# Forgetting attention: key gate sums loaded in two copies, masks filled in place, blocks 2 and 3 ahead of 0 and 1

## The chip, the cores and the metric

The kernel runs on one core of one Trainium2 chip, in one launch. The metric is the time of the device in microseconds (us). The engines are called as in the profile: PE (matrix products and transposes), DVE (vector), ACT (activations, casts), POOL (general), SP (issues transfers); PEld is PE's loading of weights.

## The reference, cut to what matters

The model has two layers on 512 tokens of width 1024, all in float32: layer 0 is a dilated attention and a gated ConvFFN, layer 1 a forgetting attention and a ConvFFN. The change lies in the forgetting attention alone. It has 16 heads of 64; keys, values and the cumulative log forget gates `c` are shared and computed once:

```python
def fox_mixer(xn, w_q, w_o, k, v, c):
    q = (xn @ w_q).reshape(B, T, B_HEADS, HEAD_DIM)
    c_t = c.transpose(0, 2, 1)
    for i in range(T // BLK):                       # T = 512, BLK = 128
        q0, q1 = i * BLK, (i + 1) * BLK
        s = jnp.einsum('bqhd,bkhd->bhqk', q[:, q0:q1], k[:, :q1]) * HEAD_DIM ** -0.5
        s = s + (c_t[:, :, q0:q1, None] - c_t[:, :, None, :q1])
        causal = jnp.arange(q0, q1)[:, None] >= jnp.arange(q1)[None, :]
        s = jnp.where(causal, s, NEG)
        p = jax.nn.softmax(s, axis=-1)
        outs.append(jnp.einsum('bhqk,bkhd->bqhd', p, v[:, :q1]))
    return jnp.concatenate(outs, axis=1).reshape(B, T, B_WIDTH) @ w_o
```

The term `c[q]` is the same for all keys of a query's row, so a softmax over the row does not depend on it.

## The kernel before

Every product of two float32 matrices is made of three products of high and low parts (`mm3`, three matmuls at lines 292, 293 and 294: high with high, low with high, high with low). The order of the instructions on each engine is the order in which the program writes them; semaphores are put in between by dependences, and tiles come from pools with a fixed number of buffers (`t4` tiles of 4 KB per partition, `t2`, `t8`, and `bank`, the eight banks of PE's accumulators). A tile whose slot is still in use makes its writer wait.

Ahead of the attention the gates are summed to `c` (16 heads by 512 keys, times 8) and stored in the chip's memory as `cd` by POOL. Four transposes on PE (`cq_ps`, L1798) and a copy on DVE turn `c` to `cq`, the query's sum with the query on the partition. For each pair of heads j = 0 to 7, SP loads the two rows of `cd`, repeated on all 128 partitions, as `ck` (`load_ck`).

The attention is a loop over 16 iterations m and two more to drain it. An iteration handles two of the four query blocks of one head pair: `pairs` is (j, 0), (j, 2) for j = 0 to 7. Blocks 0 and 1 (called light here: 128 and 256 keys) are the even iterations, blocks 2 and 3 (heavy: 384 and 512 keys) the odd ones. It is a pipeline of three iterations:

- iteration m: `f_scores` (PE, tile `s_ps`, L1833), then for each block and head in `f_exp` one DVE reduction that adds the bias and takes the minimum (L1841), and ACT's exponential (L1843); `f_norm` divides by the sums on DVE (L1853);
- iteration m + 1: `f_transpose` (PE, tile `pT_ps`, L1865; ACT copies it to `pT`, L1867);
- iteration m + 2: `f_pv` (PE, tile `o_ps`, L1880), and for a pair's second half `f_out_high` (ACT) and `f_out_low` (DVE).

`f_bias(j, i)` makes the bias of a block on POOL, one iteration ahead: two TENSOR_SCALAR (L1814, one for each head) write `cq - ck` to a new `t4` tile, and one AFFINE_SELECT (L1815) fills the upper triangle of the last 128 columns with a large negative number. The reduction, the exponential and the normalisation then work in place in that tile.

Between these steps stand other works with a place of their own by m:

- `q_part`: two projections of six matmuls in each iteration, for the queries of pairs j + 1 and j + 2; `q_high` (ACT) and `q_low` (DVE) split the result in the even iterations;
- the weights of the queries and of the output projection: `W.high` (ACT cast), `W.low` (DVE difference, L69); for the queries' weights the low part is made by ACT's negative high part (L62, at an even iteration's end) and an accumulating transfer on POOL's queue (`low_added`, L86, in the odd iteration);
- `sums_between`: loads, four DVE differences and a store of `dsums` for the ConvFFN behind it;
- from m = 13 on, `po.both`: the first matmuls of the output projection.

Of the kernel before, what the change touches and what calls it, by code (L numbers as in the profile page):

```python
# [9 lines left out]
F32 = mybir.dt.float32  # L10
# [3 lines left out]
ALU = mybir.AluOpType  # L14

D = 1024
T = 512
# [6 lines left out]
NEG = -1e30  # L24
BIG = 3.0e38
# [83 lines left out]
def trunk_kernel(ctx, tc, x, norm_gains, w_qkv_a, w_o_a, w_q_b, w_o_b, kv_norm, w_kvf, b_f,  # L109
                 w_up, conv_w, conv_b, w_down, rope, out):  # L110
    nc = tc.nc
    act, dve, pool, pe, sp = nc.scalar, nc.vector, nc.gpsimd, nc.tensor, nc.sync
# [5 lines left out]
    sml = ctx.enter_context(tc.tile_pool(name="sml", bufs=6))  # L118
    psp = ctx.enter_context(tc.tile_pool(name="psp", bufs=8, space=bass.MemoryType.PSUM))

    def t8(shape, dt=F32, name="t8"):
        return p8.tile(shape, dt, tag="t8", name=name)

    def t4(shape, dt=F32, name="t4"):
        return p4.tile(shape, dt, tag="t4", name=name)

    def t2(shape, dt=F32, name="t2"):
        return p2.tile(shape, dt, tag="t2", name=name)

    def bank(shape, name="bank"):  # L130
        return psp.tile(shape, F32, tag="ps", name=name)

    def small(n, name):
        return sml.tile([128, n], F32, tag=name, name=name)
# [95 lines left out]
    W = Weights(nc, new_raw, lambda: t8([128, 2, 1024], F32R, name="w"), pieces)  # L230
# [39 lines left out]
    for b in range(1, 4):  # L270
# [5 lines left out]
    ident = cst.tile([128, 128], F32, name="ident")  # L276
# [11 lines left out]
                       fill=NEG, base=0, channel_multiplier=-1)  # L288
    pool.affine_select(mask0[:, 128:256], mask0[:, 128:256], pattern=[[-1, 128]], compare_op=ALU.is_ge,
                       fill=NEG, base=0, channel_multiplier=1)  # L290
# [76 lines left out]
    def xs(xT, kc, s):  # L367
        return xT[0][kc // 4][:, kc % 4, s], xT[1][kc // 4][:, kc % 4, s]
# [1184 lines left out]
        act.copy(hi, o)  # L1553
        dve.tensor_tensor(lo, o, hi.bitcast(F32), ALU.subtract)

    c8 = []

    def gates():

        fo = bank([128, 128], name="f_ps")  # L1560
        for kc in range(KD):
            for q in range(4):
                pe.matmul(fo[32 * q:32 * q + 32], wfg[:, kc, :],
                          bd2.nT[kc // 4][:, kc % 4, q * 128:q * 128 + 128], start=kc == 0, stop=kc == KD - 1)

        zt = t2([128, 4, 128], name="z")
        z, u, e, lg = (zt[:, i] for i in range(4))
        act.activation(z, fo, AF.Identity, bias=bfc)
        yield
        dve.tensor_scalar(u, z, -1.0, None, ALU.mult)  # L1570
        dve.tensor_tensor(u, u, z, ALU.min)
        act.activation(e, u, AF.Exp)
        yield
        dve.tensor_scalar(u, e, 1.0, None, ALU.add)
        dve.scalar_tensor_tensor(e, u, -1.0, e, ALU.add, ALU.subtract)
        dve.tensor_scalar(z, z, 0.0, None, ALU.min)
        act.activation(lg, u, AF.Ln)
        dve.reciprocal(u, u)
        yield
        dve.tensor_tensor(e, e, u, ALU.mult)  # L1580
        dve.tensor_tensor(lg, lg, e, ALU.subtract)
        zz, one = t2([16, T], name="zz"), t2([16, T], name="one")
        pool.memset(one, 1.0)
        for q in range(4):
            r = slice(32 * q, 32 * q + 16)
            dve.tensor_tensor(zz[:, q * 128:q * 128 + 128], z[r], lg[r], ALU.subtract)
        yield
        c = t2([16, T], name="c8")
        dve.tensor_tensor_scan(c, one, zz, 0.0, ALU.mult, ALU.add)
        dve.tensor_scalar(c, c, 8.0, None, ALU.mult)  # L1590
        pool.dma_start(cd, c)
        c8.append(c)
        yield


# [8 lines left out]
    xTq = [], []  # L1604
    cks = {}

    def load_ck(j, queue=sp):
        t = t4([128, 2, T], name="ck")
        s = cd[2 * j:2 * j + 2, :]
        queue.dma_start(t, bass.AP(tensor=s.tensor, offset=s.offset, ap=[[0, 128], [T, 2], [1, T]]))  # L1610
        cks[j] = t

    qT = {}
    qps = {}
# [1 line left out]
    def q_part(j, i):  # L1616

        if j >= 8:
            return
        if i == 0:  # L1620
            qps[j] = (bank([128, T], name="q_ps"), [t.rearrange("p (k c) -> p k c", k=8) for t in W.get()])
        o, (wh, wl) = qps[j]
        for kc in (2 * i, 2 * i + 1):
            bh, bl = xs(xTq, kc, ALL)
            mm3(o, wh[:, kc, :], wl[:, kc, :], bh, bl, kc == 0, kc == KD - 1)
# [128 lines left out]
    for bp in range(2):  # L1754
        for s in range(2):
            t = slice(bp * 128, bp * 128 + 128)
# [17 lines left out]
    for c in range(4, 8):  # L1774
# [18 lines left out]
            next(gate)  # L1793
        if c == 6:
            next(down1)
    cqp = bank([128, 4, 16], name="cq_ps")
    for b in range(4):
        pe.transpose(cqp[:, b, :], c8[0][:, b * 128:(b + 1) * 128], ident[:16, :16])  # L1798
    cq = sml.tile([128, 4, 16], F32, tag="cq", name="cq", bufs=1)
    dve.tensor_copy(cq, cqp)  # L1800
    next(down1)
    load_ck(0)


    prob = {}

    bia = {}

    def f_bias(j, i):
        n = (i + 1) * 128  # L1810
        bias = t4([128, 2, T], name="bias")
        for hh in range(2):
            hd = 2 * j + hh
            pool.tensor_scalar(bias[:, hh, :n], cks[j][:, hh, :n], -1.0, cq[:, i, hd:hd + 1], ALU.mult, ALU.add)  # L1814
        pool.affine_select(bias[:, :, n - 128:n], bias[:, :, n - 128:n], pattern=[[0, 2], [-1, 128]],  # L1815
                           compare_op=ALU.is_ge, fill=NEG, base=0, channel_multiplier=1)
        bia[j, i] = bias

    def f_scores(j, i0):

# [14 lines left out]

    def f_exp(j, i, s):
        n = (i + 1) * 128
        p = bia.pop((j, i))
        nm, ls = small(2, "nm"), small(2, "ls")
        for hh in range(2):  # L1840
            dve.tensor_tensor_reduce(p[:, hh, :n], s[hh][:, :n], p[:, hh, :n], -0.125, BIG, ALU.add, ALU.min,  # L1841
                                     nm[:, hh:hh + 1])
            act.activation(p[:, hh, :n], p[:, hh, :n], AF.Exp, bias=nm[:, hh:hh + 1], scale=-1.0,  # L1843
                           accum_out=ls[:, hh:hh + 1])
        prob[j, i] = (p, ls)

    def f_norm(j, i):
        n = (i + 1) * 128
        p, ls = prob[j, i]
        rl = small(2, "rl")  # L1850
        dve.reciprocal(rl, ls)
        for hh in range(2):
            dve.tensor_scalar(p[:, hh, :n], p[:, hh, :n], rl[:, hh:hh + 1], None, ALU.mult)  # L1853
# [16 lines left out]
    ops = {}  # L1870
    OTb = {}

    def f_pv(j, i):
        if i == 0:
            ops[j] = bank([128, T], name="o_ps")
        o = ops[j]
        for k in range(i + 1):
            for hh in range(2):
                hd = 2 * j + hh
                pe.matmul(o[64 * hh:64 * hh + 64, i * 128:(i + 1) * 128],  # L1880
                          Vt[hd // 8][:, k, (hd % 8) * 64:(hd % 8) * 64 + 64], pT[j, i, hh][:, k, :],
                          start=k == 0, stop=k == i)
        del pT[j, i, 0], pT[j, i, 1]
# [28 lines left out]
        pool.dma_start(dT[l][j].rearrange("p (q d) -> p q d", q=2), t)  # L1912
        yield

    pairs = [(j, i) for j in range(8) for i in (0, 2)]
    po = Proj(8, 4, lambda kc: (OTb[kc // 2][:, 0, kc % 2, :], OTb[kc // 2][:, 1, kc % 2, :]))
    wo = W.n_get + 7
    fill = [(kc, b) for b in range(2) for kc in range(4)]
    W.ahead, W.ahead_dma = 1, 1
    for i in range(3):  # L1920
        q_part(1, i)
        if i == 0:
            W.split(W.n_get + 1)
    f_bias(0, 0)
    f_bias(0, 1)
    next(down1)
    M = len(pairs)
    sums, idle = {}, itertools.repeat(None)
# [4 lines left out]
    for m in range(M + 2):  # L1933
        live = m < M
        if live:
            j, i0 = pairs[m]
            if i0 == 0 and j + 1 < 8:
                load_ck(j + 1)
            s = f_scores(j, i0)
        if m >= 2:  # L1940
            ju, iu = pairs[m - 2]
            f_pv(ju, iu)
            f_pv(ju, iu + 1)
        if live:
            for a in range(2):
                f_exp(j, i0 + a, s[a])
            if i0 == 2 and j < 6:
                W.low_added()
        if m >= 2 and iu == 2:
            f_out_high(ju)  # L1950
        for a in range(2):
            i = i0 + a
            if live:
                if m + 1 < M:
                    f_bias(pairs[m + 1][0], pairs[m + 1][1] + a)
                q_part(j + 1 + (i > 0), (i + 3) % 4)
            next(sums.get((m, a), idle))
            if live:
                if i == 0:
                    q_high(j + 1)  # L1960
                f_norm(j, i)
            if 1 <= m <= M:
                f_transpose(pairs[m - 1][0], pairs[m - 1][1] + a)
            if 0 <= 2 * m + a - FILL < len(fill):
                po.both(*fill[2 * m + a - FILL])
            if live and (j, i) >= (6, 1):
                W.low()
            if live and (j, i) >= (6, 0) and W.n_split < wo + 4:
                W.high()
        if live and i0 == 0:  # L1970
            q_low(j + 1)
            if j < 6:
                W.high(minus=True)
        if live and i0 == 2 and j:
            f_out_low(j - 1)
        next(sums.get((m, 2), idle))

# [50 lines left out]
```

## Time and profile before

| | |
|---|---|
| median of 3 runs | 1092.03 us (1092.0 to 1092.61) |
| profiled execution | 1092.08 us, span 1090.3 us |
| mean granted clock of PE | 0.999 |
| busy, share of the span | PE 99%, PEld 88%, DVE 83%, ACT 69%, POOL 28% |
| moved by DMA | 250.03 MB, mean 229 GB/s |
| first scores of the loop on PE | 609.52 us |
| first matmul behind the loop on PE (`cv_ps`) | 716.30 us |

The span is what the profiler saw of one execution, and 1.8 us of that execution lie outside it. The attention loop takes 107 of the 1090 us. A row of a timeline gives start and length in us, engine, line, operation, output and inputs, and in brackets how long the engine stood idle before it and what released it. Busy time says that an engine had an instruction in hand, not that this one ran at its best speed.

### The profile page before, as it was taken

To read this page: it belongs to the slowest core of one execution; us is meant where nothing else is said; L and a number is where in the kernel's file an instruction comes from. 1 tells how busy PE (TensorE), PEld (TensorE's weight loads), DVE (VectorE), ACT (ScalarE), POOL (GpSimd) and SP (SyncE) were. 2 spreads that over 40 slices of the span, in tenths; PEclk is the share of its full clock that TensorE was granted. 3 is DMA by queue.
4 is the path that set the end of the run, shared out by engine and by line. 5 is a ranking of instruction groups with operands and counts; after the bars stand their busy time and mean duration, and the time that the engine had idled before them with its cause. 6 is when DMAs were issued, how large, how long until landed. Compare 5 with 4: busy or idle time off the path is not lost.

```text
span 1090.3 us, 20004 instructions
## 1 busy us (share of the span) xinstructions
PE 1081.9 (99%) x7184; PEld 964.7 (88%) x7184; DVE 908.7 (83%) x1510; ACT 750.9 (69%) x1290; POOL 304.5 (28%) x405
## 2 busy tenths in 40 slices
PE   9999999999999999999999999999999999999997
PEld 6988889999999998888888788789999999998886
DVE  6677768898999889997877877937898998989995
ACT  6654587778788757576565677766787878756573
POOL 4632110333333322000010667610233333322000
PEclk9999999999999999999999999999999999999999
DMA  9679895689999978894872776597689999978972
GB/s 314 137 275 407 339 238 156 145 204 233 248 227 223 258 230 319 326 319 106 213 155 78 215 228 196 159 291 185 131 206 240 241 226 239 239 228 315 343 261 77
DMA packets 198251, 250.03 MB, mean 229 GB/s; under 512 B 13888, under 2 KB 141880, under 8 KB 197640
## 3 DMA queue, kind: packets, MB, share of 16 engines
q1 hardware_dynamic: 175976, 181.86, 52.0%
q0 software_dynamic: 22176, 66.90, 28.5%
q8 instruction: 56, 0.92, 0.3%
q14 instruction: 43, 0.35, 0.1%
HBM read 170.28 MB, written 39.63 MB: 193 GB/s over the span
## 4 chain that ended last, share of the span: by engine, by line
PE 91%; DVE 4%; ACT 2%; issue 1%; DMA 0%; SPq 0%; DVEq 0%; ACTq 0%
PE up L292 12%; PE up L293 12%; PE up L294 12%; PE acc L293 7%; PE acc L292 7%; PE acc L294 7%; DVE w L843 2%; PE v_ps L292 2%; PE v_ps L293 2%; PE v_ps L294 2%; PE qk_ps L1361 2%; PE o_ps L1880 2%; PE s_ps L1833 2%; PE q_ps L292 2%; PE pT_ps L1865 2%; PE first L294 1%
## 5 line engine op out<-in xcount | busy, mean ns | idle before, releaser
L292 PE MATMUL up<-xsh,w 128*128 128x256 f32 x576 | 163.1, 283 | 0.0
L293 PE MATMUL up<-xsl,w 128*128 128x256 f32 x576 | 163.0, 283 | 0.0
L294 PE MATMUL up<-xsh,w 128*128 128x256 f32 x576 | 163.0, 283 | 0.0
L701 DVE SCALAR_TENSOR_TENSOR bb<-up,conv,bb 128x511 f32<-128x511 f32 (+1 forms) x160 | 119.4, 747 | 11.7 <-ACT bb L697 8.9
L292 PE MATMUL acc<-w 128*128 128x512 f32 (+1 forms) x311 | 120.6, 388 | 0.0
L294 PE MATMUL acc<-w 128*128 128x512 f32 (+1 forms) x311 | 120.4, 387 | 0.0
L293 PEld LDWEIGHTS up<-xsl,w 128*128 128x128 f32 x576 | 110.6, 192 | 0.1
L292 PEld LDWEIGHTS up<-xsh,w 128*128 128x128 f32 x576 | 110.6, 192 | 0.1
L294 PEld LDWEIGHTS up<-xsh,w 128*128 128x128 f32 x576 | 110.6, 192 | 0.0
L293 PE MATMUL acc<-w 128*128 128x512 f32 (+1 forms) x267 | 103.5, 388 | 0.1
L697 ACT ACTIVATE bb<-up,conv 128x512 f32<-128x512 f32 x80 | 62.3, 779 | 44.3 <-PE up L294 34.2
L770 POOL DMA_DIRECT2D w<-wraw x36 | 30.8, 857 | 164.2 <-ACT w L769 146.5
L720 POOL TENSOR_TENSOR hc<-bb 128x512 f32<-128x512 f32 x44 | 68.4, 1555 | 22.8 <-ACT bb L725 14.5
L60 ACT CAST w<-wraw 128x1024 fp32r<-128x1024 f32 x64 | 66.5, 1051 | 8.1 <-issue 3.8
L294 PEld LDWEIGHTS acc<-w 128*128 128x128 f32 x311 | 58.4, 188 | 11.9
L292 PEld LDWEIGHTS acc<-w 128*128 128x128 f32 x311 | 58.4, 188 | 11.9
L69 DVE TENSOR_TENSOR w<-wraw,w 128x1024 fp32r<-128x1024 f32 x44 | 54.3, 1249 | 10.6 <-ACT w L60 10.5
L293 PEld LDWEIGHTS acc<-w 128*128 128x128 f32 x267 | 50.1, 188 | 11.0 <-DVE w L843 0.9
L781 ACT CAST w<-wsum 128x1024 fp32r<-128x1024 f32 x36 | 37.9, 1052 | 30.2 <-DVE wsum L778 30.2
L843 DVE TENSOR_TENSOR w<-wraw,w 128x1024 fp32r<-128x1024 f32 x44 | 54.1, 1266 | 0.0
L293 PE MATMUL up<-xbl,w 128*128 128x256 f32 (+1 forms) x176 | 53.2, 303 | 0.0
L293 PE MATMUL up<-xcl,w 128*128 128x256 f32 (+1 forms) x176 | 53.2, 303 | 0.0
(348 smaller groups left out, 3482.3 us busy)
## 6 DMA issues: line engine op xcount, KB each, us to landing
wraw<-in_w_up_dram SPq DMA_DIRECT2D x144, 256.0 KB
w<-wraw POOLq DMA_DIRECT2D x56, 512.0 KB, 6.3
dT<-dsums SPq DMA_DIRECT2D x34, 512.0 KB
hD<-hc POOLq DMA_DIRECT2D x44, 256.0 KB, 6.2
dact<-hD SPq DMA_DIRECT2D x44, 256.0 KB
wraw<-dT SPq DMA_DIRECT2D x22, 512.0 KB
wraw<-in_w_down_dram SPq DMA_DIRECT2D x22, 512.0 KB
dsums<-in_w_down_dram SPq DMA_DIRECT2D x36, 256.0 KB
```

Of the source, the lines that this page charges most:

```text
L60: self.nc.scalar.copy(pair[:, 0, s], raw[:, s])
L69: self.nc.vector.tensor_tensor(pair[:, 1, s], raw[:, s], pair[:, 0, s].bitcast(F32), ALU.subtract)
L292: pe.matmul(o, ah, bh, start=first, stop=False, skip_group_check=shared)
L293: pe.matmul(o, ah, bl, start=False, stop=False, skip_group_check=shared)
L294: pe.matmul(o, al, bh, start=False, stop=last, skip_group_check=shared)
L697: act.activation(bb[:, i, :], ps, AF.Identity, bias=cp[:, 3, ch:ch + 1], scale=cp[:, 2, ch:ch + 1])
L701: dve.scalar_tensor_tensor(bb[:, i, n:], ps[:, :T - n], cp[:, 2 - n, ch:ch + 1], bb[:, i, n:], ALU.mult, ALU.add)
L720: pool.tensor_tensor(hc[c], bb[:, 0, :], bb[:, 1, :], ALU.mult)
L770: pool.dma_start(b[:, 1], r1, accum_op=ALU.add)
L781: act.copy(u[:, 0], sb)
L843: dve.tensor_tensor(w[:, 1], r, w[:, 0].bitcast(F32), ALU.subtract)
L1361: pe.matmul(o, ax(0, b, kc)[x], w[:, k, :], start=kc == 0 and x == 0 and w is wh, stop=kc == KD - 1 and w is wl)
```

## The change

The bias loses the query's sum: `cq`, its transposes and its copy are gone. `cd` is stored with the opposite sign and with each head's middle value (`mid`, the sum at key 256) taken off. Each head pair loads `ck` twice: a copy of 384 columns for the even blocks 0 and 2, and one of 512 for the odd blocks 1 and 3. `f_mask` in place of `f_bias` is the AFFINE_SELECT alone, in place in the copy's diagonal; the reduction reads the copy and writes a new `t4` tile `prob`. Since a mask spoils the copy for a later block, `pairs` is (j, 2), (j, 0), heavy blocks first; the mask of block 0 or 1 comes behind the reductions of block 2 or 3 in the same copy. `n` keeps the other works at their places by m. The bank of `o_ps` is taken at a pair's first PV, whichever block it is.

```diff
@@ -1553,8 +1553,6 @@
         act.copy(hi, o)
         dve.tensor_tensor(lo, o, hi.bitcast(F32), ALU.subtract)
 
-    c8 = []
-
     def gates():
 
         fo = bank([128, 128], name="f_ps")
@@ -1587,9 +1585,10 @@
         yield
         c = t2([16, T], name="c8")
         dve.tensor_tensor_scan(c, one, zz, 0.0, ALU.mult, ALU.add)
-        dve.tensor_scalar(c, c, 8.0, None, ALU.mult)
+        mid = sml.tile([16, 1], F32, tag="mid", name="mid", bufs=1)
+        dve.tensor_copy(mid, c[:, T // 2:T // 2 + 1])
+        dve.tensor_scalar(c, c, mid, -8.0, ALU.subtract, ALU.mult)
         pool.dma_start(cd, c)
-        c8.append(c)
         yield
 
 
@@ -1604,11 +1603,12 @@
     xTq = [], []
     cks = {}
 
-    def load_ck(j, queue=sp):
-        t = t4([128, 2, T], name="ck")
+    def load_ck(j):
         s = cd[2 * j:2 * j + 2, :]
-        queue.dma_start(t, bass.AP(tensor=s.tensor, offset=s.offset, ap=[[0, 128], [T, 2], [1, T]]))
-        cks[j] = t
+        cks[j] = [t4([128, 2, n], name="ck") for n in (T - 128, T)]
+        for t in cks[j]:
+            n = t.shape[2]
+            sp.dma_start(t, bass.AP(tensor=s.tensor, offset=s.offset, ap=[[0, 128], [T, 2], [1, n]]))
 
     qT = {}
     qps = {}
@@ -1793,28 +1793,16 @@
             next(gate)
         if c == 6:
             next(down1)
-    cqp = bank([128, 4, 16], name="cq_ps")
-    for b in range(4):
-        pe.transpose(cqp[:, b, :], c8[0][:, b * 128:(b + 1) * 128], ident[:16, :16])
-    cq = sml.tile([128, 4, 16], F32, tag="cq", name="cq", bufs=1)
-    dve.tensor_copy(cq, cqp)
     next(down1)
     load_ck(0)
 
 
     prob = {}
 
-    bia = {}
-
-    def f_bias(j, i):
-        n = (i + 1) * 128
-        bias = t4([128, 2, T], name="bias")
-        for hh in range(2):
-            hd = 2 * j + hh
-            pool.tensor_scalar(bias[:, hh, :n], cks[j][:, hh, :n], -1.0, cq[:, i, hd:hd + 1], ALU.mult, ALU.add)
-        pool.affine_select(bias[:, :, n - 128:n], bias[:, :, n - 128:n], pattern=[[0, 2], [-1, 128]],
-                           compare_op=ALU.is_ge, fill=NEG, base=0, channel_multiplier=1)
-        bia[j, i] = bias
+    def f_mask(j, i):
+        d = cks[j][i % 2][:, :, i * 128:i * 128 + 128]
+        pool.affine_select(d, d, pattern=[[0, 2], [-1, 128]], compare_op=ALU.is_ge, fill=NEG,
+                           base=0, channel_multiplier=1)
 
     def f_scores(j, i0):
 
@@ -1835,10 +1823,10 @@
 
     def f_exp(j, i, s):
         n = (i + 1) * 128
-        p = bia.pop((j, i))
+        c, p = cks[j][i % 2], t4([128, 2, T], name="prob")
         nm, ls = small(2, "nm"), small(2, "ls")
         for hh in range(2):
-            dve.tensor_tensor_reduce(p[:, hh, :n], s[hh][:, :n], p[:, hh, :n], -0.125, BIG, ALU.add, ALU.min,
+            dve.tensor_tensor_reduce(p[:, hh, :n], s[hh][:, :n], c[:, hh, :n], -0.125, BIG, ALU.add, ALU.min,
                                      nm[:, hh:hh + 1])
             act.activation(p[:, hh, :n], p[:, hh, :n], AF.Exp, bias=nm[:, hh:hh + 1], scale=-1.0,
                            accum_out=ls[:, hh:hh + 1])
@@ -1871,7 +1859,7 @@
     OTb = {}
 
     def f_pv(j, i):
-        if i == 0:
+        if j not in ops:
             ops[j] = bank([128, T], name="o_ps")
         o = ops[j]
         for k in range(i + 1):
@@ -1912,7 +1900,7 @@
         pool.dma_start(dT[l][j].rearrange("p (q d) -> p q d", q=2), t)
         yield
 
-    pairs = [(j, i) for j in range(8) for i in (0, 2)]
+    pairs = [(j, i) for j in range(8) for i in (2, 0)]
     po = Proj(8, 4, lambda kc: (OTb[kc // 2][:, 0, kc % 2, :], OTb[kc // 2][:, 1, kc % 2, :]))
     wo = W.n_get + 7
     fill = [(kc, b) for b in range(2) for kc in range(4)]
@@ -1921,8 +1909,8 @@
         q_part(1, i)
         if i == 0:
             W.split(W.n_get + 1)
-    f_bias(0, 0)
-    f_bias(0, 1)
+    f_mask(0, 2)
+    f_mask(0, 3)
     next(down1)
     M = len(pairs)
     sums, idle = {}, itertools.repeat(None)
@@ -1934,7 +1922,7 @@
         live = m < M
         if live:
             j, i0 = pairs[m]
-            if i0 == 0 and j + 1 < 8:
+            if i0 and j + 1 < 8:
                 load_ck(j + 1)
             s = f_scores(j, i0)
         if m >= 2:
@@ -1944,34 +1932,34 @@
         if live:
             for a in range(2):
                 f_exp(j, i0 + a, s[a])
-            if i0 == 2 and j < 6:
+            if i0 == 0 and j < 6:
                 W.low_added()
-        if m >= 2 and iu == 2:
+        if m >= 2 and iu == 0:
             f_out_high(ju)
         for a in range(2):
-            i = i0 + a
+            n = a + 2 * (m % 2)
             if live:
                 if m + 1 < M:
-                    f_bias(pairs[m + 1][0], pairs[m + 1][1] + a)
-                q_part(j + 1 + (i > 0), (i + 3) % 4)
+                    f_mask(pairs[m + 1][0], pairs[m + 1][1] + a)
+                q_part(j + 1 + (n > 0), (n + 3) % 4)
             next(sums.get((m, a), idle))
             if live:
-                if i == 0:
+                if n == 0:
                     q_high(j + 1)
-                f_norm(j, i)
+                f_norm(j, i0 + a)
             if 1 <= m <= M:
                 f_transpose(pairs[m - 1][0], pairs[m - 1][1] + a)
             if 0 <= 2 * m + a - FILL < len(fill):
                 po.both(*fill[2 * m + a - FILL])
-            if live and (j, i) >= (6, 1):
+            if live and (j, n) >= (6, 1):
                 W.low()
-            if live and (j, i) >= (6, 0) and W.n_split < wo + 4:
+            if live and (j, n) >= (6, 0) and W.n_split < wo + 4:
                 W.high()
-        if live and i0 == 0:
+        if live and i0:
             q_low(j + 1)
             if j < 6:
                 W.high(minus=True)
-        if live and i0 == 2 and j:
+        if live and i0 == 0 and j:
             f_out_low(j - 1)
         next(sums.get((m, 2), idle))
```

On POOL, the loop's first iterations before (`w` is a query weight's low part, `dsums` belongs to the ConvFFN behind):

```order
L654 DMA dT_76<-dsums 128x1024 x2
L1814 TENSOR_SCALAR bias<-ck,cq 128x128 x2
L1815 AFFINE_SELECT bias<-bias 128x2x128
L1814 TENSOR_SCALAR bias<-ck,cq 128x256 x2
L1815 AFFINE_SELECT bias<-bias 128x2x128
L1814 TENSOR_SCALAR bias<-ck,cq 128x384 x2
L1815 AFFINE_SELECT bias<-bias 128x2x128
L1814 TENSOR_SCALAR bias<-ck,cq 128x512 x2
L1815 AFFINE_SELECT bias<-bias 128x2x128
L86 DMA w<-wraw 128x1024
```

The same place of POOL after, with the line numbers of the changed kernel:

```order
L654 DMA dT_76<-dsums 128x1024 x2
L1804 AFFINE_SELECT ck<-ck 128x2x128 x4
L86 DMA w<-wraw 128x1024
L1804 AFFINE_SELECT ck<-ck 128x2x128 x4
L1889 DMA dsums<-in_w_down_dram 128x1024
L1890 DMA dsums<-in_w_down_dram 128x512
L1891 DMA dsums<-in_w_down_dram 128x512
L86 DMA w<-wraw 128x1024
```

Eight of twelve rows of arithmetic in a head pair leave the queue, and the transfers of `w` and `dsums` follow the four masks directly.

On PE, iterations 1 and 2 as a difference (`q_ps` is the query projection, `kst` and `qst` are keys and queries, `Vt` the values):

```order
-L1865 MATMUL pT_ps<-ident,bias 128x128 x2
+L1853 MATMUL pT_ps<-ident,prob 128x128 x6
 L292 MATMUL q_ps<-xqh_6471,w 128x512
 L293 MATMUL q_ps<-xql_6472,w 128x512
@@ -3421,7 +3420,8 @@
 L293 MATMUL q_ps<-xql_6472,w 128x512
 L294 MATMUL q_ps<-xqh_6471,w 128x512
-L1865 MATMUL pT_ps<-ident,bias 128x128 x4
-L1833 MATMUL s_ps<-kst_6046,qst 128x256 x12
-L1880 MATMUL o_ps<-pT,Vt_6323 64x128 x6
+L1853 MATMUL pT_ps<-ident,prob 128x128 x8
+L1821 MATMUL s_ps<-kst_6046,qst 128x384 x6
+L1821 MATMUL s_ps<-kst_6046,qst 128x512 x6
+L1868 MATMUL o_ps<-pT,Vt_6323 64x128 x14
```

The heavy transposes (6 and 8) now stand in the odd iteration, and the even one opens with the heavy scores and the heavy PV; the projections between them stay.

On SP's queue, where the first loads of `ck` stand (`dT_76` is a store for the ConvFFN, `wraw` a query weight):

```order
-L1610 DMA ck<-cd 128x1024
+L1611 DMA ck<-cd 128x2x384
+L1611 DMA ck<-cd 128x1024
 L654 DMA dT_76<-dsums 128x1024 x2
-L1610 DMA ck<-cd 128x1024
-L51 DMA wraw<-in_w_q_b_dram 128x8x128
-L1610 DMA ck<-cd 128x1024
```

Each load has become two, ahead of the same stores and weights.

## The prediction

> **What bounds the kernel now.** The page first: busy shares and the chain of work that ended last.
>
> ```profile
> PE 1081.9 (99%) x7184; PEld 964.7 (88%) x7184; DVE 908.7 (83%) x1510; ACT 750.9 (69%) x1290; POOL 304.5 (28%) x405
> PE 91%; DVE 4%; ACT 2%; issue 1%; DMA 0%; SPq 0%; DVEq 0%; ACTq 0%
> ```
>
> PE carries the time: 1081.9 of 1090.3 us busy, 91% of the chain. So POOL, of which the change removes most work in the attention stage, can matter only where something on PE ends up waiting for it. The next view is the windows over that stage (columns: us, then the busy time of each engine with its instruction count, granted clock, DMA share, GB/s).
>
> ```profile
> 655.00:665.00 10.00, 10.00 (x76) 8.21 (x76) 9.53 (x27) 7.06 (x21) 8.17 (x13) 1.00 0.55 147
> 695.00:700.00 5.00, 4.39 (x39) 3.20 (x38) 4.96 (x10) 2.23 (x5) 4.62 (x6) 1.00 0.25 81
> ```
>
> The clock is 1.00. In most stretches PE has no idle time at all; 0.61 us stand in 695 to 700, where DVE is saturated and POOL nearly so. But a stalled pipeline can also show as longer pieces, so I read the starts of the score matmuls on PE (start us, length, ...). The light ones (64x256) open the even iterations m = 0, 2, ...:
>
> ```profile
> 609.52 0.97 PE L1833 MATMUL s_ps<-kst,qst 64*128 64x256 f32 x12
> 618.46 0.98 PE L1833 MATMUL s_ps<-kst,qst 64*128 64x256 f32 x12
> 619.37 1.11 PE L1880 MATMUL o_ps<-pT,Vt 128*64 128x128 f32 x12
> 631.67 0.97 PE L1833 MATMUL s_ps<-kst,qst 64*128 64x256 f32 x12
> 644.73 0.97 PE L1833 MATMUL s_ps<-kst,qst 64*128 64x256 f32 x12
> 657.66 0.98 PE L1833 MATMUL s_ps<-kst,qst 64*128 64x256 f32 x12
> 670.76 0.98 PE L1833 MATMUL s_ps<-kst,qst 64*128 64x256 f32 x12
> 683.70 0.97 PE L1833 MATMUL s_ps<-kst,qst 64*128 64x256 f32 x12
> 688.52 1.49 PE L1833 MATMUL s_ps<-kst,qst 64*128 64x384 f32 x12
> 695.34 0.97 PE L1833 MATMUL s_ps<-kst,qst 64*128 64x256 f32 x12
> 697.28 0.66 PE L1880 MATMUL o_ps<-pT,Vt 128*64 128x128 f32 x8 [0.61 <-ACT pT L1867]
> 709.37 0.88 PE L1880 MATMUL o_ps<-pT,Vt 128*64 128x128 f32 x12
> 716.30 0.44 PE L626 MATMUL cv_ps<-ident,cv_rows 44*128 44x44 f32 x4
> ```
>
> From 618.46 one head pair takes 13.21, 13.06, 12.93, 13.10, 12.94 us. 12.93 comes twice, so I take it as the matmuls' own time; the excess over five pairs is 65.24 - 64.65 = 0.59 us. Pair 6 (683.70 to 695.34, 11.64) has one group of six projection matmuls less (1.4, from 622.75 to 624.14 in the chain shown below), so its floor is 11.53, excess 0.11. Pair 7 (695.34 to 709.37) takes 14.03 against 12.93, excess 1.10, of which 0.61 is the printed wait. So all that any rearrangement can take from these pairs is 0.59 + 0.11 + 1.10 = 1.80 us, plus 0.23 at the start (the first light PV, at 619.37, took 1.11, the one at 709.37 0.88).
>
> **Part by part.** (1) The query's sum goes. On PE that is one row of the chain, and on POOL two instructions per block:
>
> ```profile
> 604.92 0.35 PE cq_ps L1798 x4
> L1814 POOL TENSOR_SCALAR bias<-ck,cq 128x128 f32<-128x128 f32 (+3 forms) x64 | 44.8, 740 | 4.7 <-DMA ck<-cd 4.4 <-DMA w<-wraw 0.2
> L1815 POOL TENSOR_SCALAR_AFFINE_SELECT bias<-bias x32: 407/411/733, 608.8 to 697.6; 128x256 f32<-128x256 f32 x32
> ```
>
> The four transposes stand on PE with nothing idle beside them, so their 0.35 us come off in full: -0.35. The DVE copy of their result is replaced by a 16x1 copy far ahead of the stage, a wash. The 64 POOL operations take 44.8 us, 64 x 0.70. POOL is not among the engines of the chain above, so the direct gain is nothing; the cover is PE's own 12.93 us per pair, of which POOL's two sums and masks took some 7.2 (64 sums of 0.70 and 32 masks of 0.41 over eight pairs).
>
> (2) What the missing POOL work does to DVE. The same normalisations, beside POOL at work and after POOL's last block:
>
> ```profile
> 694.12 1.00 DVE L1853 TENSOR_SCALAR bias<-bias,rl 128x384 f32<-128x384 f32 x2
> 696.36 1.48 DVE L1853 TENSOR_SCALAR bias<-bias,rl 128x512 f32<-128x512 f32 x2
> 705.94 0.75 DVE L1853 TENSOR_SCALAR bias<-bias,rl 128x384 f32<-128x384 f32 x2
> 707.40 0.88 DVE L1853 TENSOR_SCALAR bias<-bias,rl 128x512 f32<-128x512 f32 x2
> 686.40 1.12 DVE L1909 TENSOR_TENSOR dsums<-dsums 128x512 f32<-128x512 f32 x1
> 709.52 0.69 DVE L1909 TENSOR_TENSOR dsums<-dsums 128x512 f32<-128x512 f32 x1
> ```
>
> A heavy pair of blocks loses 2.48 - 1.63 = 0.85 us of DVE beside POOL, and a sum in `dsums` 0.4. In the saturated stretch 683 to 700 one heavy pair and three such sums make about 2 us. The 0.59 us in the steady pairs are where DVE or ACT came late to a bank; with 0.85 us or more of room per pair on DVE most should go. Bounds: 0 (they have another cause) and 0.59; I take 0.45. The start's 0.23 is the first light PV right behind the transposes it needs; now the heavy scores (1.42 us instead of 0.90) stand between them, so it goes: -0.23.
>
> (3) The new order, tail included. PE's work per head pair is the same; heavy and light iterations change places while the projections, the `dsums` steps and the `W.high`/`W.low` steps keep theirs. In the chain, PE is left for long at one place, between 690 and 697.28:
>
> ```profile
> 691.16 0.68 DVE qst L1641
> ...
> 695.80 0.95 ACT w L60
> 696.75 0.49 ACT pT L1867
> ```
>
> and on DVE's timeline there stand
>
> ```profile
> 691.76 0.54 DVE L1841 CUSTOM_DVE_ANT_0 bias<-s_ps,bias 128x384 f32<-128x384 f32 x1
> ...
> 695.04 1.21 DVE L69 TENSOR_TENSOR w<-wraw,w 128x1024 fp32r<-128x1024 f32 x1
> ```
>
> DVE reaches the reductions of m = 13 (from 691.76) only behind the low query part, though their first scores began at 688.52; ACT's exponentials, a weight cast (0.95) and the copy of the transposed block follow, and PE waits. After the change the even m = 12 has the heavy work on DVE (reductions 2.36 by 691.76 to 694.12, two sums 1.4, normalisations 1.63, one weight difference 1.2, low query part 0.68: 7.3 us, against PE's 5.4, which is 6.82 for m = 13 before less one group of 1.4), and m = 13 the light. So DVE comes some 2 us late into m = 13, where before the lateness was there too and went on into m = 14. The same ACT order (cast ahead of copy) stays. Bounds of the tail's 1.21 us: all gone, or doubled by the heavier m = 12; the rows of (2) give back about 2 us of the late DVE, so I lean to a gain but leave two thirds: -0.4. The first PV of a pair, now the heavy one, waits for the bank that `f_out_low` of the pair before frees at the end of the odd iteration; the heavy scores (1.49) lie between, its DVE work is the light one's, so I price it at nothing, at most 0.3 in a pair.
>
> (4) The second copy of `ck`. Bytes per head pair go from 512 to 896 KB on SP's queue. What can suffer is the accumulating transfer of the query weights, whose issues and landing times in the stage are shown, then the first `ck` landing as POOL sees it, the projection that reads the weights (in the chain), and the stage's traffic:
>
> ```profile
> 616.29 0.90 POOL L86 DMA_DIRECT2D w<-wraw  x1 [0.79 <-ACT w L62]
> 640.88 0.88 POOL L86 DMA_DIRECT2D w<-wraw  x1 [3.42 <-ACT w L62]
> DMA to landing us min/median/max: 4.6/5.4/5.6
> ...
> 607.63 1.15 POOL L1814 TENSOR_SCALAR bias<-ck,cq 128x128 f32<-128x128 f32 x2 [4.37 <-DMA ck<-cd]
> ...
> 622.75 0.23 PE q_ps L292
> ...
> 623.22 0.24 PE q_ps L294
> ...
> 624.14 0.87 PE pT_ps L1865 x8
> ...
> DMA packets 9809, 23.37 MB, mean 195 GB/s; under 512 B 771, under 2 KB 5043, under 8 KB 9411
> ```
>
> At m = 2 the reader, the third matmul, is at 623.22, 6.9 us behind the issue, against 5.6. In the new order it comes 0.5 us later or so (heavy scores and PV ahead of it in its iteration, fewer transposes; the issue too moves, behind the heavy exponentials): 7.4. The added 384 KB (393 kB) at 195 GB/s are 2.0 us if all of them get ahead: 7.6. So 0 to 0.2 us lost once; I take 0. Later the distance is about 8.3 us (640.88 to 649.2: the reader stands 4.76 behind the even iteration's start, 618.46 to 623.22, and 644.73 less the 0.23 lost there gives 649.3) and grows by about 0.4 (heavy scores and PV ahead of the reader, a lighter iteration before), against at most 7.6: nothing. On SP the next `wraw` load stands behind both copies, which wait for slots that the reductions of the pair before free; its cast comes a pair, 13 us, later. Nothing. The first masks need both copies: 607.6 before, 2.0 later at most, and 0.9 for two masks, 610.5; the first scores, now heavy (1.49), end at about 610.6 (609.52 less 0.35, and 1.49). Covered, and the first block's transposes stand only a whole iteration later. In place, the masks of blocks 0 and 1 wait for the reductions of 2 and 3, which end 3.9 us (1.49 and 2.36) into an iteration of some 6.5; behind them in POOL's queue stand `dsums` issues that nobody needs within 10 us. Nothing.
>
> Sum: 0.35 + 0.23 + 0.45 + 0.4 = 1.43. The profiled execution took 1092.08 us (its span 1090.3 and 1.8 around it), 0.05 above the median 1092.03; 1092.08 - 1.43 = **1090.65 us**.
>
> **Rivals.** A measurement of this kernel can tell about 0.2% (2.2 us) from no change: faster is below 1089.85, slower above 1094.2.
>
> *All stalls go.* DVE's 2 us in 683 to 700 are more than the 1.21 us of stall behind them; then 0.35 + 0.23 + 0.59 + 1.21 = 2.38 come off: 1089.7, just across the bound. Against it: m = 12 is now DVE's heaviest iteration with the weight work in it. The Trainium skill, page "SBUF — State Buffer", section "SBUF: two separate sides", says that VectorE and GpSimd share a port pair as an exclusive lock for a whole instruction, the loser blocked fully. That speaks for this rival, and the trace agrees where a normalisation of 0.88 takes 1.48 beside POOL; the 32 masks that stay would still take that lock, about 0.41 us each at the median.
>
> *Nothing comes of the relief.* The steady stalls and the tail stay, since ACT's order causes them: 0.35 only, 1091.7. For it: at 697.28 the releaser is ACT, and its cast is not moved.
>
> *The other side: late weights.* If the accumulating transfer of a pair lands later than 8.7 us behind its issue, PE waits in every pair, because the projection's third matmul reads it. The decision point is 3.1 us above the stage's longest (5.6). The second copy alone gives 2.0. At one microsecond too late in five pairs, less 0.35 and 0.23, it is 1096.5. For it: rows elsewhere in the run reach 10.1 us.
>
> ```profile
> DMA to landing us min/median/max: 4.6/5.6/10.1
> ```
>
> The Trainium skill, page "Perfetto Trace Analysis", section "DMA Optimizations", says that transfers below 2 KB carry a heavy overhead, and the short copy has rows of 1.5 KB. If such a row cost as much as one of 2 KB, the estimate by that page is 2.7 us for the copy and a landing at 8.3, still short of the point; no run here shows it yet.
>
> **How the numbers follow.** Forecast (part of the stalls go): 0.53. All stalls go: 0.23, of which 0.21 falls below 1089.85. Nothing of the relief: 0.12. Late weights: 0.12, all of it slower. The rest, 0.67, is within 0.2%. The range goes from the second case with 0.3 of error, 1089.4, to the third with its tail doubled (1.2 more), 1092.9; outside are the late weights and a little at each end.
>
> **What would show it.** PE rows: no `cq_ps`; the heavy scores first at about 609.2; head pairs of 12.9 to 13.0 us from m = 2 on; the loop's end (`cv_ps`) at 714.9 instead of 716.30. DVE: heavy normalisation pairs near 1.63 us. POOL: 32 masks and nothing else but transfers. I am wrong if a wait on `w<-wraw` or on `ck` stands on PE's path, if pairs stay at 13.1 with POOL empty, or if PE stands for more than 1.2 us at m = 13 to 15.

## The result, and the profile after

The changed kernel takes 1103.05 us (median of 5 runs, 1101.87 to 1106.19) against 1092.0 before: ratio 1.0109, 95% interval [1.0098, 1.012]. It is slower by 11 us; 1090.65 was forecast, with a range to 1092.9. The profiled execution took 1106.19 us, the slowest of the five; its span is 1104.4.

The page of the changed kernel, the busy shares and the chain:

```profile
PE 1085.7 (98%) x7180; PEld 966.0 (87%) x7180; DVE 902.7 (82%) x1510; ACT 750.2 (68%) x1290; POOL 261.6 (24%) x341
PE 50%; issue 5%; DVE 4%; DMA 3%; ACT 2%; POOL 1%; SPq 0%; DVEq 0%; POOLq 0%; ACTq 0%
```

POOL lost 43 us of work and DVE 6, as meant, and the span grew. The chain's shares add up to 65% here and to 98% before, so they can't be compared: the version with the POOL copy below, as fast as the kernel before, shows 55% for PE. The timeline of PE (start us, us) says where the time went; the heavy scores now open the even iterations, and brackets are PE's own idle time:

```profile
611.57 1.49 PE L1821 MATMUL s_ps<-kst,qst 64*128 64x384 f32 x12
621.34 1.88 PE L1821 MATMUL s_ps<-kst,qst 64*128 64x384 f32 x12
628.88 0.50 PE L294 MATMUL q_ps<-xqh,w 128*128 128x512 f32 x1 [1.71 <-DMA w<-wraw]
636.66 1.49 PE L1821 MATMUL s_ps<-kst,qst 64*128 64x384 f32 x12
650.54 1.49 PE L1821 MATMUL s_ps<-kst,qst 64*128 64x384 f32 x12
657.17 0.50 PE L294 MATMUL q_ps<-xqh,w 128*128 128x512 f32 x1 [1.19 <-DMA w<-wraw]
666.12 1.49 PE L1821 MATMUL s_ps<-kst,qst 64*128 64x384 f32 x12
679.59 1.49 PE L1821 MATMUL s_ps<-kst,qst 64*128 64x384 f32 x12
694.04 1.49 PE L1821 MATMUL s_ps<-kst,qst 64*128 64x384 f32 x12
703.43 0.44 PE L1868 MATMUL o_ps<-pT,Vt 128*64 128x128 f32 x4 [3.08 <-ACT pT L1855]
711.46 1.50 PE L1821 MATMUL s_ps<-kst,qst 64*128 64x384 f32 x12
730.40 0.44 PE L626 MATMUL cv_ps<-ident,cv_rows 44*128 44x44 f32 x4
```

The loop, first scores to `cv_ps`, takes 118.83 us instead of 106.78: 12.05 more. From 621.34 the head pairs take 15.32, 13.88, 15.58, 13.47, 14.45 and 17.42, against 12.93 (11.53 for the sixth). Behind the loop nothing changed: 374.0 us to the span's end in both. The other 2.0 of the span's 14.1 us lie in the first 20 us, where an input tile landed late in this execution; in the nine kernels below the first scores stand at 608.1 to 609.1, so that is no part of the change.

DVE, in the same timeline, stood idle ahead of the reduction of block 3 in five pairs running:

```profile
641.86 0.69 DVE L1829 CUSTOM_DVE_ANT_0 prob<-s_ps,ck 128x512 f32<-128x512 f32 x1 [3.25 <-PE pT_ps L1853]
657.45 0.69 DVE L1829 CUSTOM_DVE_ANT_0 prob<-s_ps,ck 128x512 f32<-128x512 f32 x1 [4.95 <-DMA w<-wraw]
670.92 0.69 DVE L1829 CUSTOM_DVE_ANT_0 prob<-s_ps,ck 128x512 f32<-128x512 f32 x1 [2.62 <-PE q_ps L294]
685.37 0.69 DVE L1829 CUSTOM_DVE_ANT_0 prob<-s_ps,ck 128x512 f32<-128x512 f32 x1 [3.81 <-PE pT_ps L1853]
700.33 0.69 DVE L1829 CUSTOM_DVE_ANT_0 prob<-s_ps,ck 128x512 f32<-128x512 f32 x1 [4.09 <-PE s_ps L1821]
```

That is 18.7 us. The four releasers on PE are inferred, and wrong: the program's assignment of slots tells what the reduction waits for. In these five pairs the probability tile of block 3 gets the slot of the raw weight `wraw` that the accumulating transfer (L86) reads, and DVE may not write it before that transfer has landed.

The slot is not new. Before, the bias tile of block 3 followed a raw weight in the same way, also in five pairs, though only six tiles of a head pair went through the ten `t4` slots and not seven. But there POOL wrote the tile first, some 6 us ahead of DVE's reduction (at 678.86 behind the row below), and all its waits there came to 0.15 us:

```profile
672.56 1.37 POOL L1814 TENSOR_SCALAR bias<-ck,cq 128x512 f32<-128x512 f32 x2 [0.15 <-DMA w<-wraw]
```

With POOL's sum gone, DVE is the first to write into that slot, at the moment at which ACT and PE need the result. And the transfer now lands late. POOL's issues of it, SP's beside one of them, and its landing times (us, min/median/max; six are in the loop and one behind it):

```profile
633.35 0.89 POOL L86 DMA_DIRECT2D w<-wraw  x1 [6.25 <-ACT w L62]
647.61 0.86 POOL L86 DMA_DIRECT2D w<-wraw  x1 [2.04 <-ACT w L62]
663.18 0.90 POOL L86 DMA_DIRECT2D w<-wraw  x1 [2.06 <-ACT w L62]
676.66 0.86 POOL L86 DMA_DIRECT2D w<-wraw  x1 [2.04 <-ACT w L62]
691.11 0.90 POOL L86 DMA_DIRECT2D w<-wraw  x1 [1.21 <-PE q_ps L293]
...
647.53 1.12 SPq L1611 DMA_DIRECT2D ck<-cd  x2
650.68 0.37 SPq L51 DMA_DIRECT2D wraw<-in_w_q_b_dram  x1
...
DMA to landing us min/median/max: 7.5/8.4/9.5
```

DVE's five waits end 8.5, 9.8, 7.7, 8.7 and 9.2 us behind these issues, so at the landings. Before, the landing was 4.6/5.4/5.6. Both copies of `ck` now start 0.1 to 1.2 us ahead of the transfer, because their slots come free with DVE's reductions of the light blocks; before, the one load stood 2.8 us ahead of it:

```profile
638.08 0.32 SPq L1610 DMA_DIRECT2D ck<-cd  x1
```

The Trainium skill, page "DMA: Bandwidth & Descriptors", section "Issuing engines are not separate DMA queues", says that transfers of SP and POOL run on the same 16 engines and interleave. The trace agrees: two transfers of SP's and one of POOL's, begun within 1.2 us, and 8.4 us instead of 5.4.

So the theory (A): the late landing and the slot, in which DVE now waits, together make the loss. The rivals: the added bytes alone (B) or the late landing alone (B'), by PE's own wait; the new order alone (C); the slot alone (C'); DVE's waits for masks (D).

### The profile page after: what moved, and what is told of

It is laid out like the page before. It is cut to its first block, busy times and chain, and to the rows that moved or that the text cites. A ratio compares the mean times of both kernels' runs of the same rounds, so it can differ in the third digit from the quotient of the medians.

```text
span 1104.4 us, 19908 instructions
## 1 busy us (share of the span) xinstructions
PE 1085.7 (98%) x7180; PEld 966.0 (87%) x7180; DVE 902.7 (82%) x1510; ACT 750.2 (68%) x1290; POOL 261.6 (24%) x341
## 4 chain that ended last, share of the span: by engine, by line
PE 50%; issue 5%; DVE 4%; DMA 3%; ACT 2%; POOL 1%; SPq 0%; DVEq 0%; POOLq 0%; ACTq 0%
PE acc L293 6%; PE acc L294 6%; PE acc L292 6%; PE up L292 6%; PE up L293 6%; PE up L294 6%; DMA w<-wraw 2%; DVE w L843 1%; PE k_ps L292 1%; PE k_ps L293 1%; PE k_ps L294 1%; PE v_ps L292 1%; PE v_ps L293 1%; PE v_ps L294 1%; DMA dact<-hD 1%
## 5 line engine op out<-in xcount | busy, mean ns | idle before, releaser
L1831 ACT ACTIVATE prob<-prob,nm 128x384 f32<-128x384 f32 (+3 forms) x64 | 35.3, 554 | 27.4 <-DVE nm L1829 27.4
```

## The experiments

Each is given with its median, beside a median before of 1091.7 to 1092.0 in its own group.

**Only the order.** The kernel before with `pairs` as (j, 2), (j, 0) and the conditions that go with it; bias, query's sum and `ck` as before.

```diff
-    pairs = [(j, i) for j in range(8) for i in (0, 2)]
+    pairs = [(j, i) for j in range(8) for i in (2, 0)]
-    f_bias(0, 0)
-    f_bias(0, 1)
+    f_bias(0, 2)
+    f_bias(0, 3)
...
```

> The kernel before with only the order of blocks changed (2 and 3 ahead of 0 and 1); bias, query's sum and the single copy of ck as before. Theory A (a slot cycle: in the changed kernel the probability tile of block 3 takes the slot of the raw weight that the accumulating transfer still reads, and that transfer lands late because both copies of ck are issued beside it): the order alone does not bring the slot wait, so within 0.2% of before, 1090.5 to 1093. Theory B (the added bytes alone make the transfer late): also 1092. Theory C (heavy blocks first cost by themselves, DVE's heavy iteration meets its weight work): most of the 11 us, 1098 to 1103.

1093.73 us, ratio 1.0016 [1.0007, 1.0025], 0.7 above the range of A. C is out as the main cause. But the order is not free. On PE's timeline of this kernel, three PVs like the first below (the others at 660.20 and 686.65, 0.50 each) wait for the bank that `f_out_low` frees, and the tail for copies:

```profile
633.75 1.75 PE L1880 MATMUL o_ps<-pT,Vt 128*64 128x128 f32 x28 [0.43 <-DVE OTb L1894]
692.69 0.66 PE L1880 MATMUL o_ps<-pT,Vt 128*64 128x128 f32 x8 [0.77 <-ACT pT L1867]
699.58 0.96 PE L1833 MATMUL s_ps<-kst,qst 64*128 64x512 f32 x5 [0.82 <-ACT pT L1867]
```

**Only the traffic.** The kernel before, and beside each load of `ck` the rows of 384 once more into a spare tensor in memory.

```diff
         queue.dma_start(t, bass.AP(tensor=s.tensor, offset=s.offset, ap=[[0, 128], [T, 2], [1, T]]))
+        queue.dma_start(spare, bass.AP(tensor=s.tensor, offset=s.offset, ap=[[0, 128], [T, 2], [1, 384]]))
```

> The kernel before with 384 KB more traffic beside each load of ck, from the same rows into a spare tensor that nobody reads; no slot and no order changes. Theory A: the accumulating transfer lands at most 1.5 us later than its 5.4, PE does not wait for it: 1092 to 1093.5. Theory B: landing 7.5 us or more, and most of the loss is here: 1097 to 1103. Theory C: 1092.

1094.5 us, 1.0023 [1.0014, 1.0032]: between the two expectations. The bytes, issued 2.8 us ahead of the transfer as before, do delay it by 2.7 us, as B had it, but PE waits for it in four places by 1.9 us together (total us, times, longest). POOL waits too, in five places, since its sum for block 3 here writes the slot of the raw weight:

```profile
DMA to landing us min/median/max: 7.1/8.1/9.0
PE q_ps L294 <- DMA w<-wraw: 1.9, 4, 0.8
POOL bias L1816 <- DMA w<-wraw: 12.1, 5, 2.9
```

So a landing of 8.1, with the slot behind it as well, costs 2.5 us and not 11 where the one who waits for the slot is POOL, ahead of DVE's need.

**The short copy made on POOL.** The changed kernel, with 512 KB per pair by DMA as before; masks and order as changed. POOL writes the short copy later than the load did, and with that the tiles take other slots, which the expectation did not see: from pair 2 on a raw weight follows the raw weight, and no tile of block 3 follows one.

```diff
-        for t in cks[j]:
-            n = t.shape[2]
-            sp.dma_start(t, bass.AP(tensor=s.tensor, offset=s.offset, ap=[[0, 128], [T, 2], [1, n]]))
+        sp.dma_start(cks[j][1], bass.AP(tensor=s.tensor, offset=s.offset, ap=[[0, 128], [T, 2], [1, T]]))
     def f_mask(j, i):
+        if i == 2:
+            pool.tensor_copy(cks[j][0], cks[j][1][:, :, :T - 128])
```

> The changed kernel with the 384-column copy made on POOL from the 512-column one, so 512 KB per head pair come by DMA as before; slots and order stay. Theory A: the landing falls from 8.4 to about 6.5 us, the slot wait stays but shorter: 1095 to 1100. Theory B: the loss goes, 1091 to 1093. Theory C: 1101 to 1104.

1090.67 us, 0.9991 [0.9981, 1.0]. The loss is gone, below what A gave. The landing is back at 4.9/5.3/6.4, but the wait in the slot went with it, so this version does not tell what either is worth alone. No run has DVE in that slot behind a transfer that lands in time. An estimate: had the five transfers of the changed kernel landed 5.4 us behind their issues instead of at the ends of DVE's waits, and nothing else moved, 1.7 of DVE's 18.7 us would be left. PE's timeline of the version with the POOL copy:

```profile
617.90 1.49 PE L1821 MATMUL s_ps<-kst,qst 64*128 64x384 f32 x12
682.58 1.49 PE L1821 MATMUL s_ps<-kst,qst 64*128 64x384 f32 x12
689.71 0.66 PE L1868 MATMUL o_ps<-pT,Vt 128*64 128x128 f32 x8 [0.45 <-ACT pT L1855]
696.11 0.96 PE L1821 MATMUL s_ps<-kst,qst 64*128 64x512 f32 x5 [0.33 <-ACT pT L1855]
714.58 0.44 PE L626 MATMUL cv_ps<-ident,cv_rows 44*128 44x44 f32 x4
```

Five pairs in 64.68 us, 12.94 each: the steady stalls of before have gone.

**Light probabilities in the 2-KB pool.** The changed kernel with all its loads; five tiles per pair in the `t4` slots.

```diff
-        c, p = cks[j][i % 2], t4([128, 2, T], name="prob")
+        c, p = cks[j][i % 2], t4([128, 2, T], name="prob") if i >= 2 else t2([128, 2, 256], name="prob")
```

> The changed kernel with the probabilities of blocks 0 and 1 (at most 2 KB per partition) in the 2-KB pool, so five instead of seven tiles per head pair go through the ten 4-KB slots; all loads, masks and the order stay. Theory A: the reductions no longer wait for the transfer's landing, and the loads of ck are issued earlier than the transfer: 1090.5 to 1092.5. Theory B: the bytes stay, 1099 to 1103. Theory C: the order stays, 1099 to 1103.

1093.24 us, 1.0013 [1.0004, 1.0023], 0.7 above A's range. All 896 KB come, but earlier: the loads of `ck` are issued at 635.95, the transfer at 642.72, and it lands at 5.5/5.6/7.6. So with the loads 6.8 us ahead the bytes do not delay it: their moment counts. The one late landing (7.6) is at pair 1, where the loads of `ck` begin 1 us behind it, and PE waits 0.86 there.

**The same, with the loads put beside the transfer.** ACT issues them behind its negative high part.

```diff
-    def load_ck(j):
+    def load_ck(j, queue=sp):
...
-            if i0 and j + 1 < 8:
-                load_ck(j + 1)
+            if i0 and j == 0:
+                load_ck(1)
                 W.high(minus=True)
+                load_ck(j + 2, act)
```

> As the version with the light probabilities in the 2-KB pool, but both loads of ck are issued by ACT right behind its negative high part, so beside the accumulating transfer, as they fall in the changed kernel. No probability tile follows a raw weight in its slot. Theory A (late landing and slot together make the loss): the transfer lands at 7.5 to 9 us, PE alone waits for it, 1 to 3 us in all: 1092.5 to 1096. Theory B' (the landing alone makes the loss, by PE's own wait): 1099 to 1104. Theory C' (the slot alone, the landing is normal wherever ck is issued): landing 5.6, 1091 to 1093.

1093.66 us, 1.0018 [1.0009, 1.0027]. The landing is 5.3/7.0/8.8 (the loads stand 2 to 3 us ahead, so the collision is weaker than in the changed kernel), PE waits once, 2.06 us at pair 1, and from 635.35 the pairs take 12.94, 12.93, 12.94, 12.93. A landing of 7.0, short of the 7.5 that A wanted, without the slot: no loss per pair.

**Only the slot.** The changed kernel; the slot for the next raw weight is taken between the tiles of blocks 2 and 3. Every engine and queue has the same instructions in the same order.

```diff
             for a in range(2):
+                if a and i0 and j < 6:
+                    W.load(W.n_split + 1 + W.ahead_dma)
                 f_exp(j, i0 + a, s[a])
```

> The changed kernel with one thing moved: the slot of the next raw query weight is taken between the tiles of blocks 2 and 3, so from pair 2 on the raw weight follows the raw weight in its slot and the probability tile of block 3 follows that of the pair before. The instructions of every engine and queue keep their order; both loads of ck still wait for the light reductions and start beside the accumulating transfer. Theory A (late landing and slot together make the loss): landing 7 to 9 us as in the changed kernel, but DVE no longer waits for it; only PE's own waits and pair 1 stay: 1092.5 to 1096. Theory B' (the landing alone, by PE's own wait): 1100 to 1104. Theory D (the loss is DVE's wait for the masks or the order, not the slot): 1100 to 1104.

1099.26 us, 1.0066 [1.0049, 1.0083]: outside A's range and below the others'. The trace says why. The landing is as late as in the changed kernel. From 634.25 four pairs take 13.25, 12.93, 12.93 and 13.24, since DVE does not wait for the transfer there. Landing, masks and order are those of the changed kernel, so neither the landing alone (B') nor the masks (D) makes its loss per pair. In two places a probability tile still follows a raw weight (pairs 1 and 6), and there DVE waits and PE loses:

```profile
DMA to landing us min/median/max: 7.6/8.3/10.5
625.58 0.69 DVE L1829 CUSTOM_DVE_ANT_0 prob<-s_ps,ck 128x512 f32<-128x512 f32 x1 [4.54 <-issue]
694.06 0.69 DVE L1829 CUSTOM_DVE_ANT_0 prob<-s_ps,ck 128x512 f32<-128x512 f32 x1 [5.49 <-issue]
697.15 0.70 PE L1868 MATMUL o_ps<-pT,Vt 128*64 128x128 f32 x4 [4.23 <-ACT pT L1855]
```

**The slot in pairs 2 to 6.** With this no probability tile follows a raw weight that the transfer still reads.

```diff
             for a in range(2):
+                if a and i0 and 2 <= j < 7:
+                    W.load(W.n_split + 1 + W.ahead_dma)
                 f_exp(j, i0 + a, s[a])
```

> The changed kernel with the raw weight's slot taken between the tiles of blocks 2 and 3 in pairs 2 to 6, so no probability tile of the loop waits for the accumulating transfer; engines and queues keep their order. In the version before this one two such places were left (pairs 1 and 6), with DVE idle for 4.5 and 5.5 us there. Theory A: landings of 7.5 us and more stay, DVE's waits go, PE waits only at pair 1's weights and in the tail by less than a microsecond each: 1091.5 to 1094.5. If the late landing itself is the loss: 1097 to 1103.

1098.61 us (1093.74 to 1100.64), 1.0055 [1.0035, 1.0075]: a miss for A again. DVE's waits for the transfer have gone and the pairs take 12.9 to 13.8, but in pair 6 the slot now belongs to a raw weight of the output projection. Its load waits for the landing, ACT's cast for the load, and PE for the copies behind the cast:

```profile
681.36 0.89 POOL L86 DMA_DIRECT2D w<-wraw  x1 [3.27 <-ACT w L62]
690.10 3.48 SPq L51 DMA_DIRECT2D wraw<-in_w_o_b_dram  x3
696.07 1.05 ACT L60 CAST w<-wraw 128x1024 fp32r<-128x1024 f32 x1 [4.37 <-DMA wraw<-in_w_o_b_dram]
699.77 0.88 PE L1821 MATMUL s_ps<-kst,qst 64*128 64x384 f32 x6 [2.54 <-ACT pT L1855]
```

Whoever comes next in that slot in time pays for the landing; with slack behind it (the next query weight, pairs 2 to 5, or POOL's bias tile in the version with only the traffic) nobody does.

**The tail, and the best version once more.** The first kernel is the POOL copy with both weight casts and differences of an iteration behind its copies and normalisations; the second is the POOL copy unchanged.

```diff
+        for n in (2 * (m % 2), 2 * (m % 2) + 1):
             if live and (j, n) >= (6, 1):
                 W.low()
             if live and (j, n) >= (6, 0) and W.n_split < wo + 4:
                 W.high()
```

> The version with the short copy made on POOL, and in the last pairs both weight casts of an iteration behind both copies of transposed blocks (ACT), both weight differences behind both normalisations (DVE). If the tail's stalls of 0.45 and 0.33 us are the cast ahead of the copy, they go: 1089.8 to 1090.3, 0.5 to 0.8 below that version. If DVE's lateness makes them, no change: 1090.7.

> The version with the short copy made on POOL once more, with more rounds, to settle whether it beats before: 1090.3 to 1091.0, ratio 0.9985 to 0.9992.

1090.84 us (0.9992 [0.9983, 1.0001]) and 1090.86 (0.9994 [0.9985, 1.0003]): the same, and the second ratio just misses its range. The 0.45 at a PV goes, and 0.66 appears at the next transposes behind `f_out_low`, which points to DVE's lateness as the limit:

```profile
699.18 0.44 PE L1853 MATMUL pT_ps<-ident,prob 128*128 128x128 f32 x2 [0.66 <-DVE OTb L1882]
```

The POOL copy beats the changed kernel by 12 us and has a median 1.0 to 1.4 below before, at the edge of what two sets of runs can tell.

## Why the prediction was wrong

- **(4), the second copy, is the step that failed: it had the wrong waiter.** It held the transfer's landing against one reader, PE's third matmul, and found 7.6 against 8.7: "nothing". PE's own waits for it are 3.1 us in the changed kernel. But the tile of block 3 lies in the raw weight's slot, and DVE, now its first writer, waits 18.7 us there. PE then waits 6.4 us for ACT's copies of the transposed blocks, and through the next L62 the next transfer was pushed back as well. Neither (4) nor (1), which took POOL's sums away at no price, asked who had written that slot before, and how long ahead.
- **(4) also made the landing too short.** It gave 5.6 + 2.0 = 7.6, and 7.5 to 9.5 was measured. At the old moment of issue the added traffic alone brought 8.1 in one kernel, and loads 2 to 3 us ahead 7.0 in another. Nor did the step ask when the copies would be issued, though it said what frees their slots: the light reductions, at about the time of the cast that releases the transfer. Before, most of these slots came free with PE's transposes of an earlier block.
- **The rival "late weights" named the right transfer and the wrong waiter.** The landing's median, 8.4, is below its point of 8.7, and PE's own waits make 3.1 us of a loss of 11. That its 0.12 lay on the slower side is luck. Two signs of being wrong that the text named did come: PE waits on `w<-wraw`, and it stands for 3.08 us at m = 13.
- **(1), for the query's sum on PE, and (2) were right in mechanism**, as the version with the POOL copy shows: steady pairs of 12.94, no `cq_ps`, 0.35 and 0.56 us. Its heavy normalisations in m = 12 are the 1.63 us forecast:

```profile
687.77 0.75 DVE L1841 TENSOR_SCALAR prob<-prob,rl 128x384 f32<-128x384 f32 x2
688.62 0.88 DVE L1841 TENSOR_SCALAR prob<-prob,rl 128x512 f32<-128x512 f32 x2
```

- **The 0.23 at the start was counted twice**: it lies inside the first of the five pairs, whose excess of 0.59 holds it.
- **(3), the tail, had the wrong sign.** With the POOL copy the loop takes 106.45 instead of 106.78, so 0.33 less. The steady pairs give 0.56 of it. Eight transposes (0.87) move from the end of the loop into the first two iterations; counted so, these give 0.04, and the tail gives 0.27 back instead of gaining 0.4. The bank behind `f_out_low`, priced at nothing to 0.3, cost 0.5 in three pairs where POOL's work stayed (order alone).
- The forecast's total, 1090.65, is what the POOL copy measures, but not by its terms: they come to 0.68 us in the loop and ahead of it, and the medians differ by 1.0 to 1.4. The rest is not explained; first scores differ by up to a microsecond between kernels.

What stays open: how the 3 us by which the landing grows divide between bytes, the 1.5-KB rows of the short copy and the raw weight's load at 650.68, and what the slot would cost DVE with a landing in time. No run separates them.

## What to carry to other kernels

When a change makes another engine the first to write a tile, write down for the tile's slot who held it last and when that holder is done: a tile that follows the source of a transfer waits for its landing, and the engine that writes it takes everything behind it along. POOL, ahead of the need, could wait there for 12.1 us in a kernel that lost 2.5; DVE's 18.7 went with a loss of 11. When a load's slot is freed by another engine than before, find its new moment of issue and what starts in the same microsecond, before adding its bytes to an old landing time. Bytes can be moved off the queue that collides even if another engine then works more: a POOL copy of 1.1 us a pair here was worth 12, though it moved the tiles to other slots too.

## What the hardware showed that was not expected

After PE's long waits its granted clock fell, and the matmuls behind them took longer. In the windows (us, busy of each engine, clock, DMA share, GB/s) of the changed kernel, and then of the version with only the slot moved:

```profile
700.00:710.00 10.00, 5.93 (x39) 4.73 (x38) 9.49 (x27) 7.41 (x20) 2.42 (x4) 0.83 0.61 195
```

```profile
700.00:705.00 5.00, 5.00 (x23) 4.29 (x22) 4.30 (x17) 4.04 (x13) 0.00 (x0) 0.67 0.47 162
```

The stall of 4.23 us in the second ends at 697.15, and its eight PVs at 698.58 take 1.12 us against 0.66 with the POOL copy, so a wait in the tail cost more than its own length. A wait of 2.06 us in the loop had such a drop behind it too (the loads put beside the transfer, clock 0.50 from 628 to 630); behind the 1.71 us that end at 628.88 in the changed kernel the clock stayed at 1.00. And one transfer of 512 KB landed at 5.4, 7.0, 8.1 or 8.4 us (medians) in kernels that had, among other differences, other loads issued in the 3 us ahead of it.
